# One MoE transformer block on one core: place's row indices computed ahead of the fixed expert's products

## The chip, the core and the metric

The program runs on one core of a Trainium2 chip. The core has TensorE (matrix products, PE in the profile; PEld is its weight load), VectorE (DVE), ScalarE (ACT), GpSimd (POOL) and SyncE (SP); SP, ACT and POOL also issue DMAs. The metric is device time of one execution in microseconds, the median of several runs. Less is better.

## What is computed

A block with one layer: modulation, a token mixer (differential attention and a gated linear attention), a residual with layer norm, then a hierarchical mixture of experts over 1024 tokens of 1024 numbers, a second residual and layer norm. The mixer's end and the experts are what the change touches:

```python
def hier_moe(u, w_rg, b_rg, w_re, b_re, wg, wu, wd):
    g_logits = (uf @ w_rg + b_rg); g_idx = argmax(g_logits)        # 4 groups
    e_logits = (uf @ w_re + b_re).reshape(n_tok, 4, 8)
    top_v, top_i = top_k(e_logits[g_idx], 2)                       # 2 experts of 8
    weights = softmax(top_v) * g_w
    ...
    h = silu(xblk @ wg[e]) * (xblk @ wu[e])                        # 1024 -> 512
    y = h @ wd[e]                                                  # 512 -> 1024
    ...                                                            # weighted sum over a token's two experts
```

There are 32 experts, each with 6 MB of weights (wg, wu, wd). Which token goes to which expert is known only on the chip.

## The kernel before

The mixer runs first; its last step makes the rows of the eight token tiles (`out_tile`), writes them to a table in memory (`u2d`), and routes them. `out_tile` calls `norm` twice and sets the router's logits `lgt` between; `route` (L133) finds both experts of each token and each token's rank within its expert; `forced` (L184) makes the row list of expert 0.

**The fixed expert.** Expert 0 always gets 128 row places, so its list (`idx[:, 0:1]`) is known as soon as routing ends and does not depend on the other counts. POOL gathers its rows (`gather`, L374), TensorE transposes them (`x_T`, 8 transposes named `tru`), `x_small` (L398) copies them out of PSUM, and `full32` (L495) multiplies: 32 recorded products `pf` with wg and wu (each product of plain float32 is recorded twice), silu and product, 4 transposes `trf`, 16 recorded down products `ypf`. Its six weight loads (`f0`, L353) stand at the start of the stage on SP.

**The placed experts.** The other 31 are sorted by their count; rank r gets a number of row places that falls with r (256, 192, 128, 64, 32). `place` (L215), on VectorE, ranks the experts (`bigc`, `er`), finds which expert has rank r (`eqc`, `eid`, `eidi`, from which SP reads the expert's number for the weight loads), the place of every token (`cap`, `base`, `P_`, `posi`), and with 32 recorded products `ptb` on TensorE the row list of all placed experts (`rb`, `oh`, then the cast to `idx[:, NF:]`, L302). Gathers of the placed rows wait for that cast. Wide ranks ("heavy") run in `big`, with weights split in two parts (`wH` by ScalarE, `wL` by VectorE) and products `pg`, `pu`, `yp`; narrow ones ("light") in `small64` and `small32`. Two chains, heavy and light, are interleaved.

**What sets the order.** The code is written in program order, but a scheduler sorts the instructions of each engine, as far as data allows; each engine then runs its own list strictly in order. Eight 1 MB buffers hold raw weights (`raw0` to `raw7`, reused in turn, L334); a load is issued by SP when the buffer's last reader is done. Gathered rows have two buffers (`xg`), so a gather can wait for the transposes of the one before the last. `tc.issue_after(ins)` ties what is issued inside it, on the engine of `ins`, behind `ins`.

## Time and profile before

| | us |
|---|---|
| median of 3 runs | 2092.89 (2092.81 to 2093.69) |
| the profiled execution | 2089.53 |
| its span, first to last instruction | 2087.8 |
| TensorE busy | 1917.0 |
| VectorE busy | 1164.4 |
| ScalarE busy | 845.7 |
| POOL busy | 244.2 |
| mean granted TensorE clock | 0.968 of full |

All times of the rows below are from this one profiled execution, counted from the start of its span. The mixer's last products end near 1405 us, the fixed expert runs from 1426 to 1453, the placed experts from 1464 to about 2030, and the final sum and norm to the end. A busy TensorE is not one at its peak, since the clock that it is granted is either 1.2 or 2.4 GHz (0.50 and 1.00 in the profile).

### The profile page before, as it was taken

The numbers are of one execution on the slowest core, as the hardware profiler recorded it, in microseconds if no ns is written. First come the engines' busy times: TensorE is split into PE (matmuls) and PEld (weight loads), VectorE is DVE, ScalarE is ACT, GpSimd is POOL, SyncE is SP. The second block draws the span as 40 slices with busy tenths as digits, with TensorE's granted clock in tenths as the row PEclk, the third lists the DMA queues.
The fourth block names the chain that finished last, engine by engine and source line by source line (L and its number), as shares of the span: only waits on it lengthen the run. The fifth ranks groups of instructions, "written<-read, shape, count | busy, mean of one in ns | idle before, by whom it ended". The sixth has DMA issues, their size and how long they took to land. (4 is left out here: it accounts for less than half of the span.)

```text
span 2087.8 us, 29016 instructions
## 1 busy us (share of the span) xinstructions
PE 1917.0 (92%) x11019; PEld 1359.5 (65%) x11019; DVE 1164.4 (56%) x2113; ACT 845.7 (41%) x1430; POOL 244.2 (12%) x353
## 2 busy tenths in 40 slices
PE   6999999999999999999999999885999999988866
PEld 4777777777777777777777778672664555544322
DVE  7655276567656765866725566976333333444315
ACT  5321166556655664655534335431221222232202
POOL 1131200000000000000010100411011101111015
PEclk9999999999999999999999999897999999999988
DMA  7896472221222122121276735409798999999996
GB/s 272 222 236 228 150 246 91 91 86 50 77 91 86 56 95 72 47 97 52 96 261 219 230 124 193 159 31 371 299 419 315 350 364 362 360 373 409 422 378 241
DMA packets 142669, 434.45 MB, mean 208 GB/s; under 512 B 19160, under 2 KB 48472, under 8 KB 116416
## 3 DMA queue, kind: packets, MB, share of 16 engines
q1 hardware_dynamic: 99168, 350.60, 45.9%
q0 software_dynamic: 42880, 81.82, 12.3%
q8 instruction: 87, 1.43, 0.3%
q14 instruction: 54, 0.44, 0.1%
q10 hardware_dynamic: 480, 0.16, 0.0%
HBM read 359.64 MB, written 72.89 MB: 207 GB/s over the span
## 5 line engine op out<-in xcount | busy, mean ns | idle before, releaser
L1088 DVE CUSTOM_DVE_ANT_0 t<-sc,B 128x256 f32<-128x256 f32 (+7 forms) x128 | 95.7, 754 | 64.0 <-PE sc L1085 58.9
L349 DVE TENSOR_TENSOR wL<-rawr,wH 128x1024 fp32r<-128x1024 f32 x96 | 113.8, 1218 | 14.3 <-ACT wH L348 13.9
L859 PE MATMUL v<-wv,uH 128*128 128x512 f32 x256 | 103.4, 414 | 7.3 <-DVE veL L804 4.8
L1090 ACT ACTIVATE t<-t,nm 128x256 f32<-128x256 f32 (+7 forms) x128 | 98.6, 771 | 17.1 <-DVE nm L1088 16.8
L348 ACT CAST wH<-rawr 128x1024 fp32r<-128x1024 f32 x96 | 95.2, 1046 | 22.0 <-DMA rawr<-in_wd 9.3
L821 PE MATMUL g<-uH,wH_g 128*128 128x512 f32 x256 | 102.3, 400 | 1.8 <-DVE kz L1047 1.8
L860 PE MATMUL v<-wv,uL 128*128 128x512 f32 x256 | 103.0, 402 | 0.0
L861 PE MATMUL v<-wv,uH 128*128 128x512 f32 x256 | 102.6, 401 | 0.0
L822 PE MATMUL g<-uL,wH_g 128*128 128x512 f32 x256 | 101.8, 398 | 0.0
L823 PE MATMUL g<-uH,wL_g 128*128 128x512 f32 x256 | 101.7, 397 | 0.0
L533 PE MATMUL ps<-rawr,xT 128*64 128x512 f32 x176 | 82.1, 601 | 0.5 <-DMA rawr<-in_wg 0.5
L534 PE MATMUL ps<-rawr,xT 128*64 128x512 f32 x176 | 79.2, 597 | 0.7 <-DMA rawr<-in_wu 0.7
L803 ACT CAST aH<-pta 128x512 fp32r<-128x512 f32 (+1 forms) x80 | 43.4, 542 | 71.2 <-PE pta L1109 70.8
L1083 PE MATMUL sc<-sk,sq 128*128 128x512 f32 (+2 forms) x192 | 70.1, 369 | 1.2 <-DVE nm L1088 0.3
L804 DVE TENSOR_TENSOR aL<-pta,aH 128x512 fp32r<-128x512 f32 (+1 forms) x80 | 50.7, 634 | 34.7 <-ACT aH L803 33.8
L569 PE MATMUL ps<-rawr,xT 128*32 128x256 f32 x768 | 59.2, 410 | 9.1 <-DMA rawr<-in_wu 6.3
L1095 DVE SCALAR_TENSOR_TENSOR t<-t,rsum,t 128x128 f32<-128x128 f32 (+3 forms) x64 | 52.2, 816 | 27.3 <-ACT t L1094 27.0
L859 PEld LDWEIGHTS v<-wv,uH 128*128 128x128 f32 x256 | 49.1, 194 | 27.8 <-DVE veL L804 7.5
L1085 PE MATMUL sc<-kz,sq 128*128 128x512 f32 (+2 forms) x192 | 65.9, 350 | 0.0
L538 ACT ACTIVATE sg<-ps 64x512 f32<-64x512 f32 x11 | 6.5, 590 | 145.0 <-PE ps L534 145.0
L1406 PE MATMUL wba<-baH,wH_wba 128*128 128x512 f32 x128 | 50.7, 400 | 9.4 <-DVE gs L1412 8.9
L573 ACT ACTIVATE sg<-ps 64x256 f32<-64x256 f32 x12 | 4.5, 376 | 135.2 <-PE ps L569 135.1
(545 smaller groups left out, 5274.8 us busy)
## 6 DMA issues: line engine op xcount, KB each, us to landing
rawr<-in_wg SPq DMA_DIRECT2D x62, 1024.0 KB, 8.8
rawr<-in_wu SPq DMA_DIRECT2D x62, 1024.0 KB, 10.2
rawr<-in_wd SPq DMA_DIRECT2D x62, 1024.0 KB, 8.6
war<-in_w_ada SPq DMA_DIRECT2D x32, 512.0 KB, 5.9
yd<-o SPq DMA_DIRECT2D x24, 512.0 KB, 6.9
wa<-in_w_ada_sc SPq DMA_DIRECT2D x8, 1024.0 KB, 9.0
wvr<-in_wv SPq DMA_DIRECT2D x32, 256.0 KB, 3.1
wr_g<-in_wgt SPq DMA_DIRECT2D x16, 512.0 KB, 4.7
```

Source lines behind the costliest of these rows:

```text
L348: S.copy(H[:, s], raw[:, s])
L349: V.tensor_tensor(L[:, s], raw[:, s], H[:, s].bitcast(F32), op=ALU.subtract)
L533: MM(ps[0:64, :], x, a[:, s], start=k == 0, stop=k == 7)
L534: MM(ps[64:128, :], x, b[:, s], start=k == 0, stop=k == 7)
L821: MM(ps, H[:, k, :], uH[k][:, s], start=k == 0, stop=False)
L822: MM(ps, H[:, k, :], uL[k][:, s], start=False, stop=False)
L823: MM(ps, L[:, k, :], uH[k][:, s], start=False, stop=k == 7)
L859: MM(ps, uH[k][:, t], wv[c][k][:, 0, :], start=k == 0, stop=False)
L860: MM(ps, uL[k][:, t], wv[c][k][:, 0, :], start=False, stop=False)
L861: MM(ps, uH[k][:, t], wv[c][k][:, 1, :], start=False, stop=k == 7)
L1088: V.tensor_tensor_reduce(out=t[:, :n], in0=ps[:, :n], in1=B[:, 1024 - n:1024], scale=1.0, scalar=3e38, op0=ALU.add, op1=ALU.min, accum_out=nm)
L1090: S.activation(t[:, :n], t[:, :n], AF.Exp, bias=nm, scale=-1.0, accum_out=rsum[:, c:c + 1])
```

## The change

It does five things. `place` is called ahead of `full32` and of the fixed rows' transposes, and the rows' copy out of PSUM goes from VectorE to ScalarE. Inside `place` the block that finds each rank's expert (`eqc`, `eid`, `eidi`) is written behind the token places. The fixed expert's six weight loads are issued inside the block that is tied behind the gather of its rows: each buffer first gets a one-element fill on POOL (`touch`), which stands behind the gather, and the load on SP waits for that fill. The last step of `forced` writes the integer row list straight from the sum instead of by a sum and a cast. And in `norm` a caller may have a step done (`mid`) ahead of the last wide operation, which `out_tile` uses for the last step of the logits.

```diff
@@ -195,9 +195,10 @@
                 nc.tensor.matmul(pf[:, e:e + 1], oh, tk[:, i - i0, e:e + 1], start=i == i0, stop=i == i1 - 1)
-        V.tensor_tensor(self.idxf, pf, self.idxf, op=ALU.add)
-        if i1 == 8:
-            V.tensor_copy(self.idx[:, 0:NF], self.idxf)
+        if i1 < 8:
+            V.tensor_tensor(self.idxf, pf, self.idxf, op=ALU.add)
+        else:
+            V.tensor_tensor(self.idx[:, 0:NF], pf, self.idxf, op=ALU.add)
@@ -231,15 +232,6 @@
         V.tensor_reduce(er, big, axis=AX.X, op=ALU.add)
-
-        eqc = t([128, NS, NS], "eqc")
-        iN = ii[:, 0:NS]
-        V.tensor_tensor(eqc, er.unsqueeze(1).to_broadcast([128, NS, NS]),
-                        iN.unsqueeze(2).to_broadcast([128, NS, NS]), op=ALU.is_equal)
-        V.tensor_tensor(eqc, eqc, iN.unsqueeze(1).to_broadcast([128, NS, NS]), op=ALU.mult)
-        eid = t([128, NS], "eid")
-        V.tensor_reduce(eid, eqc, axis=AX.X, op=ALU.add)
-        V.tensor_scalar(self.eidi[:, NF:32], eid[0:1, :], float(NF), None, op0=ALU.add)
         cap, base = t([128, 32], "cap"), t([128, 32], "base")
@@ -280,6 +272,15 @@
         V.tensor_copy(self.posi, pos)
+
+        eqc = t([128, NS, NS], "eqc")
+        iN = ii[:, 0:NS]
+        V.tensor_tensor(eqc, er.unsqueeze(1).to_broadcast([128, NS, NS]),
+                        iN.unsqueeze(2).to_broadcast([128, NS, NS]), op=ALU.is_equal)
+        V.tensor_tensor(eqc, eqc, iN.unsqueeze(1).to_broadcast([128, NS, NS]), op=ALU.mult)
+        eid = t([128, NS], "eid")
+        V.tensor_reduce(eid, eqc, axis=AX.X, op=ALU.add)
+        V.tensor_scalar(self.eidi[:, NF:32], eid[0:1, :], float(NF), None, op0=ALU.add)
         blk, off = t([128, 8, 2], "blk", I32), t([128, 8, 2], "off", I32)
@@ -322,7 +323,7 @@
-        def load(e, which, nm, pool=None, halves=(0, 1), fixed={}):
+        def load(e, which, nm, pool=None, halves=(0, 1), fixed={}, touch=False):
@@ -333,6 +334,8 @@
                     raw = (pool or praw).tile([128, 2048], F32, tag=tag, name=f"raw{nm}_{which}{q}")
+                if touch:
+                    nc.gpsimd.memset(raw[0:1, 0:1], 0.0)
                 s = src[e:e + 1] if isinstance(e, int) else src[bass.DynSlice(e, 1)]
@@ -351,8 +354,6 @@
         sp = [phl.tile([128, 2048], F32, tag=t, name=f"rawf0s{j}") for j, t in enumerate(("wL", "wH"))]
-        f0 = [load(0, 0, "f0"), load(0, 1, "f0")]
-        f0.append(load(0, 2, "f0", fixed={0: sp[1], 1: sp[0]}))
@@ -395,12 +396,12 @@
-        def x_small(u, xg=None):
+        def x_small(u, xg=None, copy=V.tensor_copy):
             if xg is None:
             for s, pt in x_T(xg, f"u{u}"):
-                V.tensor_copy(T[:, s, :], pt)
+                copy(T[:, s, :], pt)
             return T
@@ -597,11 +598,13 @@
         xg0 = gather(idx[:, 0:1], "u0")
-        T0 = x_small(0, xg0)
+
         with tc.issue_after(self.last_gather.ins):
+            f0 = [load(0, j, "f0", touch=True) for j in (0, 1)]
+            f0.append(load(0, 2, "f0", fixed={0: sp[1], 1: sp[0]}, touch=True))
             g2_loads()
-        full32(f0, T0, yd[0:128, :])
         self.place(pc, px, ptr)
+        full32(f0, x_small(0, xg0, S.copy), yd[0:128, :])
@@ -1454,12 +1457,13 @@
-    def norm(src, dst, tmp, junk, g, b, nmu, sm, acc=None):
+    def norm(src, dst, tmp, junk, g, b, nmu, sm, acc=None, mid=lambda: None):
         G.tensor_tensor(sm[:, 1:2], sm[:, 0:1], mhalf, op=ALU.pow)
+        mid()
         V.scalar_tensor_tensor(dst, tmp, sm[:, 1:2], b, op0=ALU.mult, op1=ALU.add, accum_out=acc)
@@ -1502,8 +1506,8 @@
         V.scalar_tensor_tensor(lg, rc[:, 1, :], sm[:, 5:6], lg, op0=ALU.mult, op1=ALU.add)
-        norm(z, u2, u2, xa, rows["sc2"], rows["sh2"], sm[:, 5:6], sm[:, 6:8])
-        V.scalar_tensor_tensor(lg, lg, sm[:, 7:8], rc[:, 2, :], op0=ALU.mult, op1=ALU.add)
+        norm(z, u2, u2, xa, rows["sc2"], rows["sh2"], sm[:, 5:6], sm[:, 6:8],
+             mid=lambda: V.scalar_tensor_tensor(lg, lg, sm[:, 7:8], rc[:, 2, :], op0=ALU.mult, op1=ALU.add))
         q = nc.sync if i < 4 else G
```

On TensorE, at the end of the mixer and the start of the experts, before (`pf_...<-r_tk` is the last product of `forced`, `tru` the transposes of the gathered rows `xgu`, `pf<-rawf` the fixed expert's products, `trf` the transposes of its hidden rows, `ptb` place's products, `ypf` the down products; x8 of `ptb` are 16 in the profile):

```order
L197 MATMUL pf_12419<-r_tk_12420,r_oh_0_12423 128x1
L385 MATMUL tru_0_12484<-ident,xgu_12479 128x128 x4
L385 MATMUL tru_1_12490<-ident,xgu_12479 128x128 x4
L502 MATMUL pf<-rawf_00_12448,xT_12483 128x512 x4
L502 MATMUL pf<-rawf_01_12450,xT_12483 128x512 x4
L502 MATMUL pf<-rawf_10_12452,xT_12483 128x512 x4
L502 MATMUL pf<-rawf_11_12454,xT_12483 128x512 x4
L509 MATMUL trf<-ident,hf 128x128 x4
L301 MATMUL ptb<-rb,oh_12618 128x47 x8
L518 MATMUL ypf<-rawf0s_12447,hTf 128x512 x2
```

The same place now:

```order
L197 MATMUL pf_12419<-r_tk_12420,r_oh_0_12423 128x1
L302 MATMUL ptb<-rb,oh_12568 128x47 x8
L302 MATMUL ptb<-rb,oh_12578 128x47 x8
L386 MATMUL tru_0_12597<-ident,xgu_12468 128x128 x4
L386 MATMUL tru_1_12603<-ident,xgu_12468 128x128 x4
L503 MATMUL pf<-rawf_00_12472,xT_12596 128x512 x4
L503 MATMUL pf<-rawf_01_12475,xT_12596 128x512 x4
L503 MATMUL pf<-rawf_10_12478,xT_12596 128x512 x4
L503 MATMUL pf<-rawf_11_12481,xT_12596 128x512 x4
L510 MATMUL trf<-ident,hf 128x128 x4
L386 MATMUL tru_0_12666<-ident,xgu_12660 128x128 x4
```

Place's products moved from both sides of the down products to ahead of the fixed rows' transposes, and the first half of the first placed rows' transposes (`xgu_12660`) moved ahead of the down products.

On VectorE, inside place, before (`er` is each expert's rank, `eqc` and `eid` the expert of each rank, `base` and `cap` the start and size of its places, `xT` the fixed rows' copy):

```order
L233 TENSOR_REDUCE er<-bigc 128x31
L211 SCALAR_TENSOR_TENSOR w_gs<-xw,w_gs 128x8
L237 TENSOR_TENSOR eqc<-er,ii 128x961
L249 TENSOR_SCALAR base<-er 128x31
L251 TENSOR_SCALAR d<-er 128x31
L239 TENSOR_TENSOR eqc<-eqc,ii 128x961
L252 SCALAR_TENSOR_TENSOR base<-d,base 128x31
L253 TENSOR_SCALAR g<-er 128x31
L241 TENSOR_REDUCE eid<-eqc 128x31
L403 COPY xT_12483<-tru_0_12484 128x512
L242 TENSOR_SCALAR eidi<-eid 1x31
L254 TENSOR_TENSOR cap<-cap,g 128x31
```

The same place now:

```order
L234 TENSOR_REDUCE er<-bigc 128x31
L212 SCALAR_TENSOR_TENSOR w_gs<-xw,w_gs 128x8
L241 TENSOR_SCALAR base<-er 128x31
L243 TENSOR_SCALAR d<-er 128x31
L245 TENSOR_SCALAR g<-er 128x31
L278 TENSOR_TENSOR eqc<-er,ii 128x961
L244 SCALAR_TENSOR_TENSOR base<-d,base 128x31
L246 TENSOR_TENSOR cap<-cap,g 128x31
L280 TENSOR_TENSOR eqc<-eqc,ii 128x961
L243 TENSOR_SCALAR d<-er 128x31
L245 TENSOR_SCALAR g<-er 128x31
L282 TENSOR_REDUCE eid<-eqc 128x31
```

The two copies of the fixed rows are gone from VectorE's list, and the three wide operations of `eqc` and `eid` stand one to three rows later among the small ones.

On POOL, behind the mixer's last write to the table, before:

```order
L376 DMA xgu_12479<-u2d,idx 128x1024
L368 DMA g_12476<-rowsd 128x1024
L370 DMA g2h<-rowsd 64x512 x2
L372 DMA g2q<-rowsd 32x256 x4
L520 DMA yd<-ysf 128x1024
L376 DMA xgu_12655<-u2d,idx 128x1024
```

The same place now:

```order
L377 DMA xgu_12468<-u2d,idx 128x1024
L338 MEMSET rawf_00_12472 1x1
L338 MEMSET rawf_01_12475 1x1
L338 MEMSET rawf_10_12478 1x1
L338 MEMSET rawf_11_12481 1x1
L338 MEMSET rawf0s_12446 1x1
L338 MEMSET rawf0s_12445 1x1
L369 DMA g_12465<-rowsd 128x1024
```

Six fills stand behind the gather of the fixed rows, and the loads on SP wait for them; further on, three gathers of placed rows stand ahead of the write of the fixed expert's result (`yd<-ysf`), where before that write stood ahead of them.

## Rows read from the trace of the kernel before

**Rows 1.** The page, busy time of TensorE: us, share of the span, instructions.

```profile
PE 1917.0 (92%) x11019; PEld 1359.5 (65%) x11019; DVE 1164.4 (56%) x2113; ACT 845.7 (41%) x1430; POOL 244.2 (12%) x353
```

**Rows 2.** Waits: who waited for whom, total us, times, longest; TensorE 1850:2060, SP 1480:2060.

```profile
PE ps L569 <- DMA rawr<-in_wu: 6.3, 4, 1.8
...
SPq L337 <- PE ps L534: 51.7, 22, 27.4
```

**Rows 3.** Time order, TensorE: start, us, engine, line, operation, out<-in, count, [idle before].

```profile
1426.19 1.94 PE L385 MATMUL tru<-ident,xgu 128*128 128x128 f32 x8 [11.51 <-DMA xgu<-u2d,idx]
1428.06 14.94 PE L502 MATMUL pf<-rawf,xT 128*128 128x512 f32 x32
...
1444.35 1.88 PE L301 MATMUL ptb<-rb,oh 128*128 128x47 f32 x16
1446.05 7.11 PE L518 MATMUL ypf<-rawf0s,hTf 128*128 128x512 f32 x16
1453.00 1.88 PE L301 MATMUL ptb<-rb,oh 128*128 128x47 f32 x16
1464.51 1.94 PE L385 MATMUL tru<-ident,xgu 128*128 128x128 f32 x8 [9.63 <-DMA xgu<-u2d,idx]
1466.33 0.80 PE L422 MATMUL pg<-wH,xH 128*128 128x512 f32 x1
...
1471.18 0.39 PE L422 MATMUL pg<-wH,xL 128*128 128x512 f32 x1
...
1475.09 1.03 PE L385 MATMUL tru<-ident,xgu 128*128 128x128 f32 x8
1475.88 0.48 PE L422 MATMUL pg<-wH,xH 128*128 128x512 f32 x1
```

**Rows 4.** Time order, VectorE, from place's first wide operation to the index.

```profile
1414.79 1.15 DVE L231 TENSOR_TENSOR bigc<-key 128x961 f32<-128x961 f32 x1
...
1427.31 0.69 DVE L403 COPY xT<-tru 128x512 f32<-128x512 f32 x1 [6.47 <-PE tru L385]
1427.92 0.16 DVE L242 TENSOR_SCALAR eidi<-eid 1x31 int32<-1x31 f32 x1
...
1428.19 0.67 DVE L403 COPY xT<-tru 128x512 f32<-128x512 f32 x1
1428.79 0.17 DVE L252 SCALAR_TENSOR_TENSOR base<-d,base 128x31 f32<-128x31 f32 x1
...
1438.56 0.93 DVE L293 TENSOR_TENSOR rb<-rb,tokid 128x752 f32<-128x752 f32 x1
...
1454.92 0.20 DVE L302 CAST idx<-ptb 128x46 int32<-128x46 f32 x1 [1.03 <-PE ptb L301]
```

**Rows 5.** Stretches: busy us by engine; last three: granted clock, DMA share, GB/s.

```profile
1426.00:1426.50 0.50, 0.31 (x2) 0.34 (x3) 0.00 (x0) 0.00 (x0) 0.00 (x0) 0.50 0.98 401
1429.50:1430.00 0.50, 0.50 (x2) 0.07 (x1) 0.50 (x6) 0.00 (x0) 0.00 (x0) 0.52 1.10 303
...
1464.00:1468.00 4.00, 3.49 (x14) 2.81 (x14) 1.38 (x2) 1.17 (x2) 0.99 (x1) 0.50 0.02 9
...
1470.00:1470.50 0.50, 0.50 (x2) 0.34 (x2) 0.40 (x1) 0.50 (x2) 0.50 (x1) 0.50 0.65 262
1470.50:1471.00 0.50, 0.50 (x3) 0.38 (x2) 0.30 (x1) 0.50 (x2) 0.22 (x1) 0.56 0.02 8
```

**Rows 6.** Time order, ScalarE: the copy of the fixed expert's hidden rows.

```profile
1444.55 0.59 ACT L511 COPY hTf<-trf 128x512 f32<-128x512 f32 x1 [7.78 <-PE trf L509]
```

**Rows 7.** Instructions that read the index: landing times of all 24 gathers.

```profile
DMA to landing us min/median/max: 6.6/9.0/11.0
```

**Rows 8.** Time order, SP and POOL: first fixed weight loads; the third placed gather.

```profile
1413.41 0.81 SPq L337 DMA_DIRECT2D rawf<-in_wg  x2
...
1466.72 0.99 POOL L376 DMA_INDIRECT xgu<-u2d,idx  x1 [8.43 <-PE tru L385]
```

## The prediction

> **What bounds the kernel now.** I read the busy shares first: TensorE is busy for 92% of the span [rows 1], so what counts is where it stands still or runs at half clock. Then TensorE's and the weight queue's waits over the expert stage. TensorE waits for weights only in the last 200 us, 6.3 us on the larger row [rows 2]; the weight queue itself waits for TensorE to give a buffer back, 27.4 us in one piece [rows 2]. So through most of the stage the weight stream follows TensorE, and a step that TensorE reaches earlier is kept. The place of the change is read in the time order of TensorE from 1426 to 1476 us [rows 3], of VectorE there [rows 4], and in the granted clock [rows 5].
>
> The reader is to see two holes in TensorE. It stands 11.51 us until the fixed expert's rows have come (transposes at 1426.19), runs the fixed expert to 1453.00, does the second half of place's products, and stands 9.63 us more until the gather of the first placed rows lands (1464.51) [rows 3]. That gather can only go out when place's index is cast at 1454.92, behind the whole fixed expert, because VectorE stood 6.47 us in the middle of place for the fixed expert's transposes [rows 4].
>
> **The change part by part.** The fixed point after the change is the transposes of the third placed gather, which begin at 1475.09 before [rows 3]; from there the order is almost the same.
>
> *Start of place's products.* VectorE needs 1414.79 to 1439.49 (1438.56 + 0.93) before, 24.70 us [rows 4]. Out of this go the wait of 6.47 and the two row copies, 0.61 (1427.31 to 1427.92) and 0.60 (1428.19 to 1428.79). That leaves 17.0, so the first products can start at 1431.8. The three wide operations that find the experts' order stay inside this stretch: the new order only trades them with small ones. Writing the index without a cast and setting the logit step ahead of the wide one spare at most 0.2 us here, and the earlier gather is not waited for: 1431.7.
>
> *Place's products, now ahead of the fixed expert's transposes on TensorE.* Before, 16 rows of them take 1.70 us at full clock (1444.35 to 1446.05), 0.106 each [rows 3]. Now all 32 follow a stand of 17 us (1414.68 to 1431.7), and the granted clock is half after such a stand [rows 5]. Eight transposes take 0.79 us at full clock (1475.09 to 1475.88) and 1.82 at half (1464.51 to 1466.33) [rows 3], a ratio of 2.3; with ratios of 2 and 2.3 the 32 take 6.8 to 7.8 us. I take 7.2: done at 1438.9. The move costs this because the cover, the wait for the gather, is shorter than VectorE's chain.
>
> *Transposes and copy.* Before, 1.87 us lie between the first transpose and the first wide product (1426.19 to 1428.06) [rows 3]. ScalarE's copy out of PSUM takes 0.59 against VectorE's 0.69 [rows 4, 6]: 1.8. The wide products start at 1440.7, 12.6 us later than before.
>
> *The fixed expert's first products.* Sixteen wide ones take 6.95 us at full clock (1446.05 to 1453.00) [rows 3], so 32 take 13.9; before they took 14.9 (1428.06 to 1443.0) as the clock was half until 1429.99, 1.9 us after the first of them [rows 5]. At the second start it was half until 1470.95, 4.6 us after the first wide product [rows 5]. Half clock for 1.9 to 4.6 us costs half of that; I take the middle, 3.3, so 1.65: they end at 1456.2, 13.2 later than before.
>
> *Between the products.* ScalarE's copy of the hidden rows ends at 1445.14 before (1444.55 + 0.59) [rows 6], yet the down products start at 1446.05, because the first half of place's products stood between them [rows 3]. That 0.85 goes; the transposes of the next rows fit into the copy's time. The down products run from 1458.4 to 1465.4.
>
> *After the fixed expert.* Before, 22.09 us from 1453.00 to 1475.09: 16 of place's products, the hole of 9.63, and 16 transposes with 24 products, more than half of this last piece at half clock. Now place's products and the hole are gone: the index is there at 1439.1, the first placed gather goes out at about 1440, and TensorE wants it at 1457.6, 17 us later; the slowest of the 24 gathers landed in 11.0 [rows 7]. Eight transposes take 0.8, four more 0.4, 24 products 0.23 each (1471.18 to 1475.09 is 17 of them) 5.5 [rows 3], and 0.3 for small waits: 7.0, so 1472.4.
>
> Sum: 1475.09 − 1472.4 = **2.7 us earlier.** As terms: −9.6 for the hole, −2.7 for place's products between and behind the fixed expert's (0.85 + 1.88), −3.6 for half clock after the hole (10.58 from 1464.51 to 1475.09, now 7.0), +13.2 for the later end of the fixed expert's first products.
>
> *The weights behind the gather.* Their six issues move from 1413.41 [rows 8] to behind the gather and six one-element fills on POOL, some 3.5 us. Before, they went out 14.6 us ahead of the first wide product (1428.06); now it is 24 us (1416.9 to 1440.7), so the delay costs nothing; without that cover it would cost the 3.5. In return the gather is alone on the wires, but nobody waits for it: place's products are later. The placed experts' weights queue behind the fixed ones on SP either way, and their numbers are known at 1421 instead of 1428.
>
> *A new edge.* The third placed gather goes out only when the second four transposes of the first placed rows are done, at about 1466.0, and TensorE wants it at 1472.4. Before, it was issued at 1466.72 [rows 8] with the wires idle (share 0.02 in 1464 to 1468) and its bytes were through by 1470.5 [rows 5], 3.8 us. At that price it is hidden with 2 us to spare. The Trainium skill's page "DMA: Bandwidth & Descriptors", section Issuing engines are not separate DMA queues, says that transfers begun on different engines share the same 16 DMA engines and interleave; by that rule the gather is only that quick if the weight loads have run dry. The trace bears it out so far: beside 3.8 us with idle wires, the gathers whose landing is known needed 6.6 to 11.0. Nothing in the sum needs this sentence.
>
> **The numbers.** The profiled execution took 2089.53 us around its span of 2087.8; the median is 2092.89. I take the 2.7 off the median: **2090.2.** The comparison can tell about 0.2%, 4.2 us, from no change, that is below 2088.7 or above 2097.1.
>
> **Rivals.**
>
> *The clock rises during place's products.* At the first start before, it rose 3.8 us after the first transposes (1426.19 to 1429.99); at the second 6.4 us after (1464.51 to 1470.95) [rows 3, 5]. If it rises 3.8 us into place's products, 17 go at half and 15 at full clock (5.4 us), transposes and copy take 1.2, and all 32 wide products 13.9. They end at 1452.2 instead of 1456.2, and all shifts: 6.7 us gained, 2086.2. For it: TensorE has 32 products in a row there. Against: before both rises TensorE had run wide products for 1.9 and 4.6 us; that place's short ones bring a rise is shown nowhere in this trace. Chance 0.25.
>
> *The gain is given back at the end.* If the weight stream sets the end of the stage, the time stays at 2092.9, since the stream's last megabyte comes no sooner. For it: the waits for weights late in the stage [rows 2]. Against: the wires are idle around 1466 because all buffers are full (share 0.02) [rows 5], so the stream moves with TensorE. Chance 0.11.
>
> *The third placed gather becomes the wait.* Place: TensorE's transposes of its rows at 1472.4. If the last three weight loads, released at 1456, still run at 1466, the gather lands 6.6 to 11.0 us [rows 7] after its issue at 1466.3, at 1472.9 to 1477.3. TensorE stands 0.5 to 4.9 us and afterwards runs up to 6.4 us at half clock, another 0 to 3.2: 2090.7 to 2098.3. It decides from a landing 8.8 us after the issue, where the gain is gone; it is slower by more than 0.2% only near the upper end. Against: the loads end by about 1465 at the rate before. Chance 0.06; where it is slower, the landing is near 11.0 and most of the half clock comes on top: 2097.5.
>
> That the change does not do what it says I exclude: the order of the changed kernel has place's products ahead of the transposes.
>
> **How the numbers follow.** The forecast has 0.58. Its own range: products 6.8 to 7.8 (±0.5), clock 1.9 to 4.6 (±0.7), gather 0 to 1, other gaps late in the stage where the clock falls or holds by the moment (±1): 2088.3 to 2091.9. The range for 8 in 10 takes in most of the first rival (2086.2) and the give-back (2092.9): 2085.8 to 2093.5. Faster by over 0.2%: 0.22 of the first rival's 0.25, and 0.13 of the forecast's 0.58 (a gain over 4.2 needs both the clock and the products at their good ends), so 0.35. Slower by over 0.2%: 0.03 from the third rival and 0.01 for what I don't see, 0.04. Within 0.2%: 0.61.
>
> **What would show it.** In the time order of VectorE after: no wait inside place, the second of the products' inputs ready near 1431.7. On TensorE: place's 32 products in one run from there, at 0.2 us each or falling to 0.1 partway (first rival); the wide products starting at 1440 to 1441 (1438 in the first rival); no wait between the down products and the first placed ones; transposes of the third placed gather near 1472. Granted clock: half up to some 1443 to 1445. I am wrong if VectorE's chain ends much off 1431.7, since every microsecond there shifts the end by one; if TensorE waits for a gather or for weights behind 1465; or if the gain at 1475 is not found again at the end of the span.

## The result and the profile after

The changed kernel takes 2080.9 us (median of four runs, 2079.58 to 2081.47); four runs of the kernel before beside it took 2092.8 to 2099.0. The ratio is **0.9934, 95% interval 0.9916 to 0.9952**: 0.66% faster, where 2090.2 us and a range from 2085.8 to 2093.5 were forecast. On another chip the same two kernels gave 0.9937 (0.9919 to 0.9954). The profiled execution took 2079.58 us around a span of 2077.8, 10.0 less than the one of before.

At the transition things went as forecast, a little better. The time order of TensorE after, answering [rows 3] (start, us, engine, line, operation, out<-in, count, idle before it and what ended that):

```profile
1431.60 7.06 PE L302 MATMUL ptb<-rb,oh 128*128 128x47 f32 x32 [16.96 <-DVE rb L294]
1438.45 1.95 PE L386 MATMUL tru<-ident,xgu 128*128 128x128 f32 x8
1440.27 14.55 PE L503 MATMUL pf<-rawf,xT 128*128 128x512 f32 x32
...
1456.98 7.10 PE L519 MATMUL ypf<-rawf0s,hTf 128*128 128x512 f32 x16 [0.29 <-issue]
1463.92 1.04 PE L386 MATMUL tru<-ident,xgu 128*128 128x128 f32 x8
1464.71 0.47 PE L423 MATMUL pg<-wH,xH 128*128 128x512 f32 x1
...
1470.86 1.03 PE L386 MATMUL tru<-ident,xgu 128*128 128x128 f32 x8
```

Place's products start at 1431.60 behind a stand of 16.96 us, the hole of 9.63 us ahead of the placed rows is gone, and the transposes of the third placed gather, the forecast's fixed point, begin at 1470.86 instead of 1475.09: 4.2 us earlier. The other 5.8 us of the span arise behind this point, where the prediction expected nothing. The stretches of both kernels from 1565 to 1625 us show where most of it is (busy us and instructions of PE, PEld, DVE, ACT, POOL; then granted clock, share of the DMA engines, GB/s). Before:

```profile
1565.00:1595.00 30.00, 27.91 (x129) 15.47 (x122) 13.44 (x17) 7.31 (x10) 3.59 (x6) 1.00 0.88 323
1595.00:1600.00 5.00, 3.80 (x14) 1.42 (x11) 2.13 (x4) 2.48 (x3) 2.18 (x3) 1.00 0.89 329
1600.00:1625.00 25.00, 22.59 (x143) 12.65 (x143) 5.30 (x8) 2.66 (x5) 2.21 (x3) 0.93 0.89 311
```

After:

```profile
1565.00:1595.00 30.00, 29.51 (x129) 15.51 (x128) 13.15 (x19) 8.82 (x12) 4.23 (x5) 1.00 0.88 327
1595.00:1600.00 5.00, 5.00 (x23) 4.07 (x23) 2.83 (x3) 0.00 (x0) 1.17 (x2) 1.00 1.01 403
1600.00:1625.00 25.00, 23.29 (x161) 13.97 (x160) 5.77 (x7) 5.23 (x7) 1.98 (x4) 1.00 0.95 382
```

TensorE stands for 5.7 us of these 60 before and 2.2 after, ran at half clock for a while before and not after, and the weights' stream moves 382 GB/s instead of 311. In this stretch the third heavy expert ends and the fourth begins. Here are TensorE's row transposes there (`tru`: rows of units 5, 6 and 20), before:

```profile
1591.51 0.66 PE L385 MATMUL tru<-ident,xgu 128*128 128x128 f32 x4
1593.16 1.07 PE L385 MATMUL tru<-ident,xgu 128*128 128x128 f32 x8
1596.02 0.66 PE L385 MATMUL tru<-ident,xgu 128*128 128x128 f32 x4
1601.09 1.08 PE L385 MATMUL tru<-ident,xgu 128*128 128x128 f32 x4 [2.29 <-DMA xgu<-u2d,idx]
1604.01 0.66 PE L385 MATMUL tru<-ident,xgu 128*128 128x128 f32 x4
```

and after:

```profile
1584.64 0.66 PE L386 MATMUL tru<-ident,xgu 128*128 128x128 f32 x4
1585.37 0.60 PE L386 MATMUL tru<-ident,xgu 128*128 128x128 f32 x4
1587.20 0.60 PE L386 MATMUL tru<-ident,xgu 128*128 128x128 f32 x4
1587.87 0.60 PE L386 MATMUL tru<-ident,xgu 128*128 128x128 f32 x4
1591.05 1.07 PE L386 MATMUL tru<-ident,xgu 128*128 128x128 f32 x8 [0.49 <-DMA xgu<-u2d,idx]
```

The scheduler has written TensorE's list differently here, 120 us behind the change and in code that the diff doesn't touch. The four groups of units 5 and 6 stand close together, the buffers of the gathered rows come free sooner, and the gather for unit 20 is issued earlier. Its issue on POOL, before and after:

```profile
1594.04 1.54 POOL L376 DMA_INDIRECT xgu<-u2d,idx  x1 [10.62 <-PE tru L385]
```

```profile
1586.25 1.05 POOL L377 DMA_INDIRECT xgu<-u2d,idx  x1 [7.60 <-PE tru L386]
```

TensorE wants the rows earlier too, 4.3 us behind the issue where it was 4.8 before. So the wait of 0.49 us instead of 2.29 is not one of more room: the gather landed 4.7 us behind its issue instead of 6.9 (more on this in the last section). Behind the wait of 2.29 the clock is granted at half for 3.4 us; behind that of 0.49 it stays at full.

To compare traces two measures are used below. The **lead** is how much earlier than the kernel before a trace has moved the same number of bytes (rates of 5 us stretches added up from 1380), both counted from place's first wide operation on VectorE (1414.79 before). The **stage** is the time from that operation to the end of the span. They are needed because that operation starts anywhere from 1410.2 to 1420.9 us in twenty traces, 6.6 us apart for one and the same kernel: times of whole runs carry this, the stage doesn't. A trace is one run, though: the stage of one kernel differs by up to 6.9 us between two of its traces.

| kernel | wait for unit 20's gather, us | lead at 1535 | lead at 1625 | stage, us | ratio (95%) |
|---|---|---|---|---|---|
| before | 2.29 | 0 | 0 | 673.0 | 1 |
| before_again | 4.97 | 0.8 | −3.2 | 679.9 | one run |
| changed | 0.49 | 4.4 | 11.1 | 663.1 | 0.9934 |
| after_again | 0.52 | 3.1 | 10.1 | 665.5 | 0.9937 (0.9919 to 0.9954) |
| before_new_order | 0.45 | 0.6 | 6.4 | 666.9 | 0.9935 (0.9918 to 0.9951) |
| after_old_order | 3.25 | 4.5 | 1.0 | 676.0 | 0.9972 (0.9960 to 0.9984) |
| after_old_order_2 | 3.02 | 4.1 | 3.9 | 670.4 | one run |
| before_third_new | 6.34 | 1.3 | −3.4 | 675.8 | 1.0004 (0.9991 to 1.0017) |
| before_second_new | 2.25 | −1.5 | −0.9 | 671.4 | 0.9967 (0.9951 to 0.9982) |
| old_order_no20 | left out | 4.2 | 7.3 | 667.2 | 0.9957 (0.9939 to 0.9976) |
| new_order_no20 | left out | 4.3 | 11.8 | 659.5 | 0.9931 (0.9913 to 0.9949) |
| no_place_pin | 0.54 | 0.4 | 5.5 | 673.0 | 0.9972 (0.9959 to 0.9985) |
| no_touch_pin | 0.56 | 4.0 | 11.1 | 663.6 | 0.9921 (0.9901 to 0.9942) |
| no_scopy_pin | 0.36 | 3.0 | 9.7 | 662.7 | 0.9932 (0.9911 to 0.9953) |
| early_half | 0.64 | 5.7 | 10.8 | 666.1 | 0.9939 (0.9922 to 0.9955) |
| tail_less_products | 0.48 | 4.6 | 11.0 | 664.7 | 0.9937 (0.9920 to 0.9954) |
| tail_less_bytes | 0.60 | 4.5 | 11.3 | 659.3 | 0.9902 (0.9882 to 0.9921) |
| ps_ahead | 0.38 | 5.1 | 13.1 | 659.0 | 0.9921 (0.9901 to 0.9941) |
| ps_ahead_2 | 0.36 | 2.9 | 11.2 | 665.1 | 0.9929 (0.9904 to 0.9955) |
| early_load_ps_ahead | 0.34 | 4.3 | 12.4 | 663.0 | 0.9944 (0.9921 to 0.9967) |

### The profile page after: what moved, and what is told of

Same layout as the page of the kernel before. It is cut to its first block, busy times and chain, and to the rows that moved or that the text cites. A ratio compares the mean times of both kernels' runs of the same rounds, so it can differ in the third digit from the quotient of the medians.

```text
span 2077.8 us, 29032 instructions
## 1 busy us (share of the span) xinstructions
PE 1915.2 (92%) x11019; PEld 1362.4 (66%) x11019; DVE 1162.3 (56%) x2110; ACT 846.5 (41%) x1432; POOL 246.4 (12%) x359
## 3 DMA queue, kind: packets, MB, share of 16 engines
q0 software_dynamic: 42880, 81.82, 12.4%
## 5 line engine op out<-in xcount | busy, mean ns | idle before, releaser
L1448 PE MATMUL yo<-woH,m 128*128 128x512 f32 x128 | 52.6, 411 | 4.9 <-ACT woH L806 2.6
```

## The experiments

**Holding TensorE's order.** Most kernels below hold TensorE's list of one stretch to a given order, with edges that order the issue and add no wait. Holding by itself costs nothing that shows: no_touch_pin, no_scopy_pin and tail_less_products, below, hold the changed kernel's own order, each with one small edit more, and are as fast as it is. An entry of the table is a tile's name, which of that name, its first product and how many:

```diff
+ORDER = (
+    ('ps20', 0, 0, 18), ('pu', 2, 0, 3), ('ps20', 0, 18, 14), ('pu', 2, 3, 5), ('trh20', 0, 0, 2),
...
+        prev = None
+        for b, rank, first, count in ORDER:
+            g = groups[b][sorted(groups[b])[rank]]
+            for i in g[first:first + count]:
+                if prev is not None:
+                    tc.add_manual_dep(i, prev.name, mybir.DependencyInfo(mybir.DependencyClass.NoSync, mybir.DependencyReason.DATA), reason="order")
+                prev = i
```

**1. The changed transition with the old order (after_old_order, twice).** From ps20 (1549 us) on, the table has the order of the kernel before. At the end of the third heavy expert that is:

```diff
 ('trh10', 0, 0, 4), ('tru5_0', 0, 0, 4),
-('yp', 7, 3, 1), ('tru5_1', 0, 0, 4), ('yp', 7, 4, 6), ('tru6_0', 0, 0, 4), ('yp', 7, 10, 1), ('tru6_1', 0, 0, 4), ('yp', 7, 11, 1),
-('yp10', 0, 0, 3), ('tru20_0', 0, 0, 4), ('tru20_1', 0, 0, 4), ('yp10', 0, 3, 5), ('pg', 4, 0, 12),
+('yp', 7, 7, 5), ('tru5_1', 0, 0, 4), ('tru6_0', 0, 0, 4), ('yp10', 0, 0, 3), ('tru6_1', 0, 0, 4), ('yp10', 0, 3, 1),
+('pg', 4, 0, 4), ('tru20_0', 0, 0, 4), ('yp10', 0, 4, 1), ('tru20_1', 0, 0, 4), ('yp10', 0, 5, 3), ('pg', 4, 4, 8),
```

> The changed kernel, with TensorE's list of one stretch (from the products ps20 of the second pair of placed experts to ps16, some 900 products) held to the order that it has in the kernel before; the transition to the placed experts stays the changed one. Theory A (order): 4.2 us of the gain arise at the transition and some 6.6 us more where the new list puts the row transposes of the next heavy expert earlier (the lead over the kernel before goes from 4.2 to 5.9 us near 1565 us and to 10.7 us near 1605 us); with the old order they are lost: 2087.5 us, between 2085 and 2090 since clock falls later move it by 3. Theory B (early start): the lists are as good as each other and the weights' stream, which starts its unbroken stretch earlier, gives the rest by itself: 2081 us, within 1.

> The changed transition with the old order once more, for a second trace: the first was among the slowest two of its ten runs (2094.7 us; median 2089.6). If the old order gives the transition's 4.2 us back at the gather near 1600 us in every run, this trace shows a wait of 2 us or more there and 673 us or more from the start of the placement to the end. If the first trace was an exception, it shows 668 to 670 us, the kernel before's 673.0 less the transition's gain.

2089.6 us (median of ten runs, 2086.1 to 2095.3) where the kernel before took 2094.7: ratio 0.9972. More than half of the gain is gone, as theory A has it. In both traces the lead of 4.1 to 4.5 us that the transition makes doesn't grow behind 1535; in the first it is lost. The wait is back:

```profile
1601.38 1.09 PE L443 MATMUL tru<-ident,xgu 128*128 128x128 f32 x4 [3.25 <-DMA xgu<-u2d,idx]
```

The second trace has the wait too (3.02 us), but its stage, 670.4, is close to what was expected if the first were an exception (668 to 670): part of the transition's gain gets through in some runs.

**2. The old transition with the new order (before_new_order).** The kernel before, same stretch, the order of the changed kernel (the diff above with its signs turned).

> The kernel before, with TensorE's list of the same stretch (ps20 to ps16) held to the order that it has in the changed kernel; the transition stays the old one. Theory A (order): 6.6 us faster than the kernel before: 2086.7 us, between 2084 and 2089.5. Theory B (early start): no change, 2093 us within 1.

Ratio 0.9935 (2083.1 against 2094.7 us), as large as the whole change's. The order is real and enough; theory B falls. It was also undersized: 11.6 us where 6.6 were expected, of which the trace's stage shows 6.1 against the first trace of before and 13.0 against the second.

So the two gains don't add up in the times. The transition alone has 0.9972 and the order alone 0.9935, together that would be 0.9907; the changed kernel has 0.9934, and 0.9937 in after_again, which was run to tell this (0.9915 or lower if they add up, 0.993 to 0.9945 if they overlap). On the traces the changed kernel's stage is 1.4 to 3.8 us shorter than the one here, and the intervals leave room for that. Why the transition brings so little on top of the new order is not shown.

**3. Only its later half (before_third_new).** The table starts at trh10.

> The kernel before, with TensorE's list held to the order of the changed kernel only from the transposes trh10 on, that is in the stretch where the third heavy expert ends and the fourth begins (1584 to 1606 us); what stands ahead of it stays as before. If the four row transposes that stand ahead of the fourth expert's products there, in place of a wait of 2.3 us for a gather and of 4 us at half clock, are what the order is worth, this gives most of it: 5 us of 11, 2088 to 2089 us where the kernel before takes 2093. If the order's worth lies in the stretch before (1549 to 1570 us), it gives 2 us at most.

Nothing: 1.0004. The 5 us expected first failed to come; "2 us at most" fits. The transposes do stand as in the changed kernel, and TensorE wants the rows 4.3 us behind the gather's issue as it does there, but the gather lands later (landing time of this gather, then TensorE's row):

```profile
DMA to landing us min/median/max: 10.5/10.5/10.5
```

```profile
1604.32 1.94 PE L435 MATMUL tru<-ident,xgu 128*128 128x128 f32 x8 [6.34 <-DMA xgu<-u2d,idx]
```

In the changed kernel the same gather landed after 4.7 us:

```profile
DMA to landing us min/median/max: 4.7/4.7/4.7
```

**4. Only its earlier half (before_second_new).** The new order from ps20 up to trh10, the old one from there.

> The kernel before, with TensorE's list held to the order of the changed kernel only in the stretch from ps20 to the products ahead of the transposes trh10 (1549 to 1584 us); from trh10 on the list is the one of before. The new order of both stretches gave a ratio of 0.9935, that of the later stretch alone 1.0004. If the earlier stretch is worth its own part (its two gaps of 1.7 and 0.4 us, and the moments at which it sets the loads and the gathers that follow), it gives the rest: 8 us or more, 2083 to 2086 us where the kernel before takes 2094. If both have to come together, because the gather for the fourth heavy expert is what is waited for and lands after 4.6 us only when it is issued early and into a stream that stands, then this order alone gives 2 us (its own gaps), 2091 to 2093 us, and the trace shows that wait again at 1600 us.

0.9967 in the times, but its runs lie in two groups (six from 2083.0 to 2086.6, six from 2090.6 to 2092.5), and its traced run began the stage 4.6 us earlier than the kernel before; from there it shows a lead that grows by 0.6 us between 1535 and 1625, a wait of 2.25 and a stage of 671.4. The trace says that the halves have to come together; the times leave room for a part of its own.

**5. The gather left out, in both orders (old_order_no20, new_order_no20).** Both leave out unit 20's gather and its transposes.

```diff
+                    if u == 20:
+                        TS[u, n] = TS[19, n]
                     if (u, n) not in TS:
```

> The changed kernel with TensorE's list of ps20 to ps16 in the order of the kernel before, leaving out one gather and its eight transposes: light experts 21 to 24 multiply the rows of the unit before. That gather is what TensorE waits for near 1600 us (2.3 us in the kernel before, 3.3 us in the old order behind the new transition, 6.3 us with the later stretch alone new), and behind that wait it runs at half clock for 3.4 us and more. If that wait is what the old order costs, this kernel is within 1.5 us of the next one (new order, the same left out), and from the start of the placement to the end it takes 661 to 664 us, where the old order took 676. If the old order costs elsewhere (a gap of 1.7 us at 1570 us and loads that wait longer for their buffers), it stays 4 us or more slower than the next one.

> The control: the changed kernel with its own order and the same gather and eight transposes left out. There the gather landed after 4.7 us and TensorE waited 0.5 us. Eight transposes are 1.1 us: 1 to 2 us faster than the changed kernel, 662 to 663 us from the start of the placement to the end, where the changed kernel took 663.1 and 665.5.

Without that gather the old order gains 3.1 us between 1535 and 1625 (4.2 to 7.3), where after_old_order's two traces lost 3.5 and 0.2 with it; the new order gains 7.5. So the wait is a part, not all: the old order's stage is still 7.7 us longer than its control's. By the same leads 4.4 us of this arise between 1535 and 1625 (7.5 less 3.1). There the old order stands 1.7 us for `hL` and 0.3 for `sg` ahead of the down products, and its clock was lower from 1568 to 1598:

```profile
1568.00:1598.00 30.00, 27.91 (x112) 14.98 (x110) 12.19 (x16) 5.42 (x8) 3.06 (x5) 0.94 0.79 296
```

The control from 1565 to 1595:

```profile
1565.00:1595.00 30.00, 29.32 (x130) 15.84 (x129) 14.17 (x19) 9.80 (x13) 3.22 (x4) 1.00 0.89 340
```

**6. The parts of the transition, under one order (no_place_pin, no_touch_pin, no_scopy_pin).** Each undoes one part; the order from ps8 to ps16 is held to the changed kernel's.

```diff
+        T0 = x_small(0, xg0, S.copy)
...
+        full32(f0, T0, yd[0:128, :])
         self.place(pc, px, ptr)
-        full32(f0, x_small(0, xg0, S.copy), yd[0:128, :])
```

> The changed kernel without the move of the placement: in the code the fixed expert's products stand ahead of it again; its weights are still loaded behind the gather and ScalarE still copies its rows; TensorE's list from ps8 to ps16 is held to that of the changed kernel. If the place of the placement on TensorE is what the transition gives, this kernel is 4.2 us slower than the changed one, if the gains add up, and the same as the kernel before with the new order (ratio 0.9935). If the transition's gain comes from the weights behind the gather (its rows land after 5.7 us in place of 11.0), it is as fast as the changed kernel, within 1 us.

Without place ahead the transition gives nothing (lead 0.4 at 1535), and the hole is back behind the fixed expert:

```profile
1455.76 1.88 PE L366 MATMUL ptb<-rb,oh 128*128 128x47 f32 x16
1468.92 1.94 PE L450 MATMUL tru<-ident,xgu 128*128 128x128 f32 x8 [11.29 <-DMA xgu<-u2d,idx]
```

On the trace the order's gain comes (5.1 us from 1535 to 1625) but doesn't last: 2.2 us of lead are left at 1895, and the stage, 673.0, is no shorter than the kernel before's. The ratio, 0.9972, shows less than half of before_new_order's gain, though both have the new order behind an old transition. These runs don't explain that; by this kernel the transition is worth 0.35% on top of the new order, by before_new_order nothing.

```diff
         sp = [phl.tile([128, 2048], F32, tag=t, name=f"rawf0s{j}") for j, t in enumerate(("wL", "wH"))]
+        f0 = [load(0, 0, "f0"), load(0, 1, "f0")]
+        f0.append(load(0, 2, "f0", fixed={0: sp[1], 1: sp[0]}))
...
-            f0 = [load(0, j, "f0", touch=True) for j in (0, 1)]
-            f0.append(load(0, 2, "f0", fixed={0: sp[1], 1: sp[0]}, touch=True))
```

> The changed kernel with the fixed expert's weights loaded ahead of the gather again, as before; TensorE's list from ps8 to ps16 is held to that of the changed kernel. The fixed expert's rows are needed at 1438.45 us only, and landed at 1426 in the kernel before. If the late weights do nothing for the time here: as the changed kernel, within 1.5 us. If they cost (the stream starts 3.5 us later): 2 to 3.5 us faster than the changed kernel. If the gather's early landing is worth something: up to 4 us slower.

```diff
-        full32(f0, x_small(0, xg0, S.copy), yd[0:128, :])
+        full32(f0, x_small(0, xg0, V.tensor_copy), yd[0:128, :])
```

> The changed kernel with VectorE copying the fixed expert's rows, as before (two copies of 0.45 us); TensorE's list from ps8 to ps16 is held to that of the changed kernel. With the placement ahead, VectorE is free when the rows are transposed (1438.5 to 1440.4 us), so the copies stand in nobody's way: as the changed kernel, within 1.5 us. Rival: they stand ahead of the cast of the index (1438.70) and hold back the first gather, 1 to 2 us slower.

Both kernels, no_touch_pin and no_scopy_pin, are as fast as the changed one within their intervals (0.9921 and 0.9932), with leads of 4.0 and 3.0 at 1535 and stages of 663.6 and 662.7. Neither the late weights nor ScalarE's copy is worth anything measurable once place is ahead.

**7. The stand ahead of place's products used (early_half).** TensorE's order: transposes, a quarter of the wide products, then place's.

```diff
+        T0 = x_small(0, xg0, S.copy)
         self.place(pc, px, ptr)
-        full32(f0, x_small(0, xg0, S.copy), yd[0:128, :])
+        full32(f0, T0, yd[0:128, :])
...
-    ('ptb', 0, 0, 16), ('tru0_0', 0, 0, 4), ('tru0_1', 0, 0, 4), ('pf', 0, 0, 8), ('pf', 1, 0, 8),
+    ('tru0_0', 0, 0, 4), ('tru0_1', 0, 0, 4), ('pf', 0, 0, 4), ('ptb', 0, 0, 16), ('pf', 0, 4, 4), ('pf', 1, 0, 8),
```

> The changed kernel with the fixed expert's row transposes and a quarter of its gate and up products (8 of 32 recorded) ahead of the placement's products on TensorE, the rest of TensorE's list held as it is. In the changed kernel TensorE stands from 1414.7 to 1431.6 us although the fixed expert's rows land at 1420.8 us. If TensorE's lead at the third placed gather still decides (theory A), the products that move into the stand bring 5 to 9 us there: 2072 to 2076 us. If the weights' stream decides (theory C), what can be won is what the stream stands still between 1465 and 1480 us (shares 0.82, 0.50, 0.76: 4.6 us of 15): not below 2076 us. If the placement's products come later by the quarter (they start at half clock, 7.2 us for 8), the index is later and the gain under 2 us: 2079 to 2081 us.

TensorE does reach the first placed products 5.6 us earlier, counted from the stage's start (1460.71 here, 1464.71 in the changed kernel, whose stage starts 1.64 earlier). Place's products are not later for it (16.95 us behind the stage's start, 16.85 in the changed kernel), so the last of the three reasons above is not the one. It is the third placed gather that is late, 8.5 us behind its issue:

```profile
1433.34 4.48 PE L370 MATMUL ptb<-rb,oh 128*128 128x47 f32 x32 [2.22 <-DVE rb L362]
1437.61 13.20 PE L571 MATMUL pf<-rawf,xT 128*128 128x512 f32 x24
...
1469.42 1.14 PE L454 MATMUL tru<-ident,xgu 128*128 128x128 f32 x8 [2.41 <-DMA xgu<-u2d,idx]
```

Nothing is left of it at the end (0.9939).

**8. What sets the end (tail_less_products, tail_less_bytes).** Both work on light experts 26 to 29. The first leaves out three quarters of their gate and up products, the second one of each expert's two down loads (4.19 MB in all).

```diff
-                    MM(ps[g * 32:g * 32 + 32, :], x, ab[g // 2][:, o:o + 256], start=k == 0, stop=k == 7)
+                    if not (26 <= r < 30 and 0 < k < 7):
+                        MM(ps[g * 32:g * 32 + 32, :], x, ab[g // 2][:, o:o + 256], start=k == 0, stop=k == 7)
```

> The changed kernel, leaving out three quarters of the gate and up products of four of the last light experts (the first and the last of eight blocks are kept): 96 products fewer on TensorE in the last 150 us, with all weights loaded as before. If the stream of weights sets the end of that stretch, no change beside the changed kernel, within 1 us. If TensorE's chain sets it, 96 products at 0.1 us are up to 10 us.

```diff
-            d = [half(2, 0), half(2, 1)]
+            d = [half(2, 0)] * 2 if 26 <= r < 30 else [half(2, 0), half(2, 1)]
```

> The changed kernel, leaving out the second half of the down weights of four of the last light experts (the first half is used twice), so that the weights' stream is 4.19 MB shorter in the last 150 us and TensorE's work is the same. Theory C (the stream, which moves 420 GB/s without a pause from 1885 to 2028 us, sets the end): 4.19 MB at 420 GB/s are 10.0 us: 2071 us, between 2070 and 2073. Rival (TensorE's chain sets the end of that stretch, and the stream runs ahead of it): 2080 to 2081 us.

Fewer products change nothing (0.9937, the changed kernel's ratio); TensorE waits for weights instead:

```profile
1988.61 0.63 PE L635 MATMUL ps<-rawr,xT 128*32 128x256 f32 x4 [1.76 <-DMA rawr<-in_wg]
1991.01 0.63 PE L635 MATMUL ps<-rawr,xT 128*32 128x256 f32 x4 [1.77 <-DMA rawr<-in_wu]
1993.98 1.07 PE L635 MATMUL ps<-rawr,xT 128*32 128x256 f32 x4 [2.35 <-DMA rawr<-in_wg]
```

Fewer bytes bring 0.32 to 0.35% more than the changed kernel, some 7 us of the 10.0 expected; the intervals just meet, so the size is rough. The stream does set the end of the last 150 us; that 3 us don't arrive is not settled. This is its stretch in the changed kernel:

```profile
1885.00:2015.00 130.00, 107.22 (x696) 50.43 (x698) 44.90 (x71) 22.57 (x30) 14.10 (x25) 0.93 1.01 421
```

**9. A faster version (ps_ahead twice, early_load_ps_ahead).** Five groups of a heavy expert's products go behind a light expert's last ones, and the list is held down to the last light expert. One of the groups:

```diff
-    ('pg', 5, 12, 12), ('ps21', 0, 18, 14), ('trh21', 0, 0, 2),
+    ('pg', 5, 12, 5), ('ps21', 0, 18, 14), ('pg', 5, 17, 7), ('trh21', 0, 0, 2),
```

> The changed kernel, with five groups of TensorE's products moved: for light experts 21, 11, 14 and 25 seven, for 15 three products of the heavy expert that stand ahead of the light expert's last products stand behind them, so that SiLU and the product of ScalarE and VectorE have cover (TensorE waits 0.94, 1.41, 1.41, 1.04 and 1.47 us there). If TensorE's waits ahead of 1885 us decide when the stream of weights runs through, 5.5 us of them go and the time falls to 2075 to 2077 us where the changed kernel takes 2082. If the light products then wait for their own weights, or the stream stands less but is full anyway, nothing: 2081 to 2083 us.

> The five moved groups of products once more, beside another set of runs of the kernel before: the first time the ratio was 0.9921 and the stage took 659.0 us, 5 less than the changed kernel's 663 to 666. If the moved groups are worth 5 us in the stage in every run, it takes 657 to 661 us again and the ratio is 0.991 to 0.9925; if the first trace was a lucky one, 663 us and 0.9935.

> Two steps in one: the five moved groups of products (ratio 0.9921) and the fixed expert's weights loaded ahead of the gather as before (0.9921, against 0.9936 for the changed kernel). If both are real and add up: a ratio of 0.9905, some 2074 us. If the early load is only noise between chips, 0.992.

0.9921 and 0.9929 against 0.9934 and 0.9937: lower both times, but inside the intervals, and the second stage (665.1) is no shorter than the changed kernel's. With the early load on top it was 0.9944, so the two don't add up. A version that beats the changed kernel is not shown.

**10. The kernel before once more (before_again).**

> The kernel before once more, for a second trace of its stage of experts. In the first it took 673.0 us from the start of the placement to the end; the changed kernel's two traces took 663.1 and 665.5. If the stage's length is a matter of the program and not of the run, this one takes 671 to 675 us, with a wait of 2 us or more for the gather near 1600 us, whatever the moment at which the stage starts (it lay between 1410 and 1421 us in the traces so far).

The stage took 679.9 us, outside the 671 to 675 expected and 6.9 longer than in the first trace, with this wait:

```profile
1603.20 1.09 PE L385 MATMUL tru<-ident,xgu 128*128 128x128 f32 x4 [4.97 <-DMA xgu<-u2d,idx]
```

So the trace on which the prediction rested was a good run of the kernel before, 3.4 us under the median shown.

## Why the prediction was wrong

The step that failed is the sentence on the fixed point, **"from there the order is almost the same"**, with what hangs on it: a shift at 1475 that is carried 1:1 to the end. From 1549 to 1606 us the order is not the same, and that reorder alone is worth more (0.9935) than the transition alone (0.9972). In the 12 traces with the new order and the gather the lead grows by 5.1 to 8.3 us between 1535 and 1625, whatever the transition; in the six with an old half or both it changes by −4.7 to +0.6. The wait for unit 20's gather is 0.34 to 0.64 us in the former and 2.25 to 6.34 in the latter. The lists of both kernels could be compared ahead of the result, down to this stretch; a moved transpose there should have been looked at like one at the transition. Its price could hardly have been read from them: with the same list from trh10 on, before_third_new gains nothing, since its gather lands late. Why the whole new order goes with early landings is open. So is how far a shift is carried: with the old order, 1.9 us of a lead of 4.1 are left at 1895 in one trace, and in the other the lead of 4.5 has turned into 1.9 behind.

*Place on VectorE.* Right: the second input of the products was ready at 1431.5 (1430.61 + 0.93), forecast 1431.7.

*Place's products.* Right: 32 in one run from 1431.60, 7.06 us (7.2 forecast), at half clock to the end. The first rival, a clock that rises among them, is refuted here.

*The wide products.* Start 1440.27 (1440.7 forecast). The half-clock term was mis-sized: 3.3 us were taken, between 1.9 and 4.6, and it was 1.2:

```profile
1426.00:1441.00 15.00, 9.40 (x41) 8.89 (x42) 8.75 (x19) 1.15 (x2) 1.39 (x2) 0.50 1.01 389
1441.00:1441.50 0.50, 0.50 (x2) 0.25 (x1) 0.00 (x0) 0.02 (x1) 0.50 (x1) 0.56 1.02 426
1441.50:1456.00 14.50, 13.71 (x35) 5.95 (x35) 5.41 (x5) 5.75 (x6) 0.20 (x1) 1.00 1.02 420
```

The clock rises at 1441.4, 1.2 us into them; that is 1.0 us of the 1.5 by which the transition was better than forecast (1470.86 against 1472.4), and the rest is the 0.4 at their start. The term changes from run to run: the clock rose some 3.5 us into the wide products in after_again and ps_ahead_2, 0.7 to 1.6 in the other eleven traces that have all of place's products ahead of all wide ones. That it came early in the first trace is luck.

*Between the products.* Right: the down products start 0.10 us behind the end of the copy (1456.30 + 0.58), where 0.91 lay before.

*The third placed gather.* No wait in the changed kernel: issued at 1464.80, it landed after 4.8 us, with the DMA engines' share at 0.73 to 0.97 in stretches of 2 us from 1464 to 1470. So a gather can be quick without idle wires, other than the prediction has it. Its bounds were thin too: [rows 7] and the prediction speak of all 24 gathers, but the trace of before gives the landing of ten; in the changed kernel it gives all 24, 4.4 to 11.6 us. The third rival's mechanism is real. It appeared in early_half, at the size given (2.41 us, in a range of 0.5 to 4.9; a landing after 8.5 us, share 1.01 from 1461 to 1471), as soon as TensorE came 5.6 us sooner.

*The weights behind the gather and ScalarE's copy.* Costed at nothing, and nothing they are (no_touch_pin, no_scopy_pin).

*The give-back.* Half right. The stream sets the end of the last 150 us, as that rival says (tail_less_products). But it doesn't swallow the gain. The likely reason, which no run tests by itself, is that it stands still further up and stands less when TensorE is ahead. From 1465 to 1480 us, before:

```profile
1465.00:1480.00 15.00, 15.00 (x65) 10.52 (x65) 8.68 (x10) 6.24 (x8) 2.98 (x3) 0.80 0.34 103
```

and after:

```profile
1465.00:1480.00 15.00, 15.00 (x73) 8.49 (x72) 7.80 (x9) 5.66 (x8) 4.30 (x4) 1.00 0.69 230
```

Of the lead at 1850 us (11.8) 8.7 are left where the stream becomes full (1895), and these 8.7 stay to 2015 without a change of more than 0.2.

*The clock elsewhere.* "±1" for late gaps was too narrow: the same program's stage differs by 2.4 us (changed), 5.6 (after_old_order), 6.1 (ps_ahead) and 6.9 (before) between two traces. The forecast's own range, 2088.3 to 2091.9, is also narrower than its terms: added up they reach from 2088.0 to 2093.4.

For the transition alone the mechanism was right and the size somewhat low. Counted from place's first wide operation, the transposes of the third placed gather begin after 58.7 to 60.5 us in the six traces with place behind, and after 55.8 to 57.2 in the thirteen with all of it ahead: 3.5 us earlier on the mean, where 2.7 were forecast and the first pair of traces has 4.2. With the old order behind it, after_old_order's ratio of 0.9972 is a gain of 5.9 us (3.3 to 8.4); 2.7 lies just below that interval.

## What to carry to other kernels

Where a scheduler writes the lists, compare them over the whole stage and look at each place where a wait's producer moves, however far behind the edit; a change at one place may be paid for at another. Hold the lists to tell the two apart: the list alone gave no price here. A lead can be kept where what it runs into (here the weights' stream) still stands somewhere ahead, so read that stream's share by stretches before carrying a shift to the end. And take two traces of the kernel before: one trace's wait of 2.29 us was 4.97 in the next.

## What was not expected of the hardware

The same kind of gather (128 rows of 4 KB) landed after 4.6 us (before_new_order) and 4.7 (changed, both traces), 6.9 and 9.6 (before, twice), 7.2 (before_second_new), 7.9 and 7.7 (after_old_order, twice) and 10.5 (before_third_new), with the DMA engines' share, in stretches of 2 us around it, at 0.66 to 1.12 in before_new_order and the changed kernel and 0.81 to 1.11 in before and before_third_new. In these two quick cases the next 1 MB load was issued some 2.5 us behind the gather, in both traces of before and in before_third_new 0.7 to 1.1 us behind it. That fits the Trainium skill's page "DMA: Bandwidth & Descriptors", section Issuing engines are not separate DMA queues, by which such transfers share the same 16 engines; it was not tested by moving that load, and in after_old_order both loads had long been issued, in before_second_new 0.8 us ahead of the gather. The cause of the landing times stays open.

The granted clock stayed at 0.50 through all 32 of place's products and the eight transposes behind them, 8.7 us in which TensorE hardly paused (1431.60 to 1440.27), and rose 1.2 us into the wide products. In none of the thirteen traces with all of place's products ahead did it rise before the wide products. What sets that moment is not shown.
